# Where the weights of each TensorE pass stand in SBUF, modulo 256 bytes

## The chip, the cores and the metric

The kernel runs on one core of a Trainium2 chip. The metric is the device time of one execution in microseconds; before the change the median of three runs is 2378.27 us (2377.22 to 2378.45).

## The reference

Two layers of an encoder over 512 tokens of width 1024, all in float32. Each layer is a half-step SwiGLU, a mixer with three branches (chunked attention, pooling, forgetting attention), and a second SwiGLU; shift, scale and gate of each come from a vector `c`.

```python
for l in range(DEPTH):
    mod = (c_act @ w_ada[l] + b_ada[l]).reshape(B, N_MOD, D_MODEL)
    h = modulate(rms_norm(x, norm_gain[l, 0]), mod[:, 0], mod[:, 1])
    x = x + 0.5 * mod[:, 2][:, None, :] * swiglu(h, ffn_w_gate[l, 0], ffn_w_up[l, 0], ffn_w_down[l, 0])
    h = modulate(rms_norm(x, norm_gain[l, 1]), mod[:, 3], mod[:, 4])
    x = x + mod[:, 5][:, None, :] * hybrid_mixer(h, w_in[l], qk_gain[l], rel_bias[l], forget_bias[l], ...)
    h = modulate(rms_norm(x, norm_gain[l, 2]), mod[:, 6], mod[:, 7])
    x = x + 0.5 * mod[:, 8][:, None, :] * swiglu(h, ffn_w_gate[l, 1], ffn_w_up[l, 1], ffn_w_down[l, 1])
```

`swiglu(h, g, u, d)` is `(silu(h @ g) * (h @ u)) @ d` with an inner width of 2816.

## The kernel before

**Numbers in two halves.** Every float32 operand of a large product is split into a high half `hi` (a cast to the format that TensorE multiplies) and a low half `lo` (what the cast left over). A product is then three passes into the same accumulator: weights' hi by moving hi, weights' hi by moving lo, weights' lo by moving hi (L119 to L121 in `triple`, L128 to L130 in `add_product`). A pass is one load of 128 columns of weights and one matmul, with 512 moving columns ("wide") or 256 ("narrow").

**Weight chunks.** `wchunk` loads 512 KB of weights into a `raw` buffer (SP's queue), ACT casts them into `hi` (L291), and DVE subtracts to get `lo` (L293; at the very start POOL does). `hi` and `lo` come from two tags, `whi` and `wlo`, three buffers each, used in turn. At the boundary between two phases some chunks are fetched early into `ptb` or `b` buffers instead.

**Feed-forward.** Part of each gate and up product is formed wide, directly from chunks (`unit`). The rest is done two blocks at a time by `seven`, a scheme that needs seven products of quarter blocks in place of eight, all narrow: each has 12 passes. The blocks A11, A12 and A22 are split into `whi`/`wlo` buffers, and the sums and differences S1 to S4 into `ptb` buffers. In order the products are A11, A12, S2, S1, S3, S4, A22, so that over successive `seven` calls 36 passes with weights in `whi`/`wlo` alternate with 48 with weights in `ptb`. There are 70 calls. The down product runs through `k_outer` in wide passes, except for the last half of each phase, which runs in narrow ones, one half of the tokens after the other, so that the next norm can begin; the mixer's output product does the same.

**Mixer.** Query, key and value projections have the activations `hhi`/`hlo` as weights and the weight chunk as the moving operand, wide. In the attention, `weigh` (L1023, L1024) has the values (`xv`, `v2`) as weights and the transposed probabilities (`pta`, `ptb`) moving, narrow for the most part. `merge_units` and `pool_in` run wide from chunks.

**Order of the work.** PE's order is that in which the code emits its passes. Norm pieces, scheduled block sums and attention steps are put among them by `later` and `poll`, at counts of passes. On the other engines a scheduler orders the instructions within what their dependencies allow, and tags with a fixed number of buffers decide when a load or a cast may begin.

**Places in SBUF.** The table gives where the tiles of each tag begin in a partition, modulo 256 bytes, in the built program. A slice of 128 or 256 float32 columns steps by 512 or 1024 bytes, so all weights and moving slices of a tile share its value.

| Tag | before | after |
|---|---|---|
| `hhi`, `hlo`, `b`, `xv`, `v2` | 0 | 0 |
| `whi`, `wlo` (before), `w` (after) | 0 | 0, or 224 for slices taken with `NARROW` |
| `ptb` | 32 | 224 |
| `pta` | 96 | 32 |

The "distance" of a pass is the address of its weights minus that of its moving operand, modulo 256.

Of the kernel before, what the change touches and what calls it, by code (L numbers as in the profile page):

```python
# [15 lines left out]
F32 = mybir.dt.float32  # L16
F32R = mybir.dt.float32r
# [23 lines left out]
def encoder_kernel(tc, xT, c, w_ada, b_ada, gains, w_gate, w_up, w_down, w_qkv, w_f, w_ubg,  # L41
# [21 lines left out]

    def st(shape, dt, tag, bufs):
        return sb.tile(shape, dt, tag=tag, bufs=bufs, name=nm(tag))

    def acc(shape=(P, T)):
        return ps.tile(list(shape), F32, tag="acc", bufs=4, name=nm("acc"))
# [72 lines left out]
    nc.scalar.dma_start(crow, c)  # L141
    nc.scalar.activation(crow, crow, AF.Silu)
    x_blocks, squares, crows = [], [], []
    for b in range(4):
        xb = blk("xv", F32)
        nc.sync.dma_start(xb, xT[:, 2 * b:2 * b + 2, :])
        x_blocks.append(xb)
        sq = st([P, 2, T], F32, "wlo" if b else "whi", 3)
        for a in range(2):
            nc.scalar.activation(sq[:, a, :], xb[:, a, :], AF.Square)  # L150
        squares.append(sq)
        if b < 2:
            pc = mmt()
            mm(pc, ones[0:1, :], crow[:, b * T:(b + 1) * T], start=True, stop=True)
            crows.append(pc)
# [34 lines left out]
            yield  # L190


    modc = cp.tile([P, L, 9, KD], F32, name="modc")
    apre = cp.tile([P, L, 3, KD], F32, name="apre")

    def mod_step(l, j, d, tag="raw"):
        raw = st([P, D], F32, tag, {"v2": 4, "raw": NRAW, "b": NB}[tag])
# [75 lines left out]
                mod_credit[0] -= 1.0  # L273
                mod_pop()

    def wchunk(src, shape, side=True, spare=None, lo_eng=None):
        lo_eng = lo_eng or nc.vector
        side_work(side)
        raw = st([P] + list(shape), F32, *(("b", NB) if spare else ("raw", NRAW)))
        last["dma"] = nc.sync.dma_start(raw, src).ins  # L280
        if spare == "ptb":
            both = st([P, 2] + list(shape), F32R, "ptb", 2)
            hi, lo = both[:, 0], both[:, 1]
        elif spare == "b":
            hi = st([P] + list(shape), F32R, "b", NB)
            lo = st([P] + list(shape), F32R, "b", NB)
        else:
            hi = st([P] + list(shape), F32R, "whi", 3)
            lo = st([P] + list(shape), F32R, "wlo", 3)
        with behind("scalar"):  # L290
            nc.scalar.copy(hi, raw)  # L291
        with behind("vector"):
            lo_eng.tensor_tensor(lo, raw, hi.bitcast(F32), op=ALU.subtract)  # L293
        return hi, lo
# [107 lines left out]
    def k_outer(chunk_src, nch, lhs_rhs, before_last=None):  # L402

        if before_last is None:
            parts, nheld = [(None, slice(0, T), [acc() for _ in range(4)])], 2
        else:
            parts = [(hs, slice(hs * HALF, (hs + 1) * HALF), [b((P, HALF)) for _ in range(4)])
                     for hs, b in enumerate((mmt, acc))]  # L410
            nheld = 3

        def go(part, j, chunks):
            _, cols, accs = part
            for c, hi, lo in chunks:
                for kk in range(2):
                    a, b, x, y = lhs_rhs(hi[:, kk, :], lo[:, kk, :], 2 * c + kk, j)
                    triple(accs[j], a, b, x[:, cols], y[:, cols], start=(c == 0 and kk == 0),
                           stop=(c == nch - 1 and kk == 1))

        held = []
        for c in range(nch):
            if before_last is not None:
                if c == nch - 2:
                    quiet[0] = 8
                    before_last()
                quiet[0] = 8
            hi, lo = wchunk(chunk_src(c), (2, T))
            if c < nch - nheld:
                for part in parts:  # L430
                    for j in range(4):
                        go(part, j, [(c, hi, lo)])
            else:
                held.append((c, hi, lo))
        if before_last is not None:
            quiet[0] = 5
        for part in parts:
            for j in range(4):
                go(part, j, held[:-2])
            for j in range(4):  # L440
                go(part, j, held[-2:])
                yield j, part[0], part[2][j]
# [79 lines left out]
    def seven(srcs, blocks, bank):  # L522

        raws = []
        for src in srcs:
            side_work()
            raw = st([P, KD, P], F32, "raw", NRAW)
            last["dma"] = nc.sync.dma_start(raw, src).ins
            raws.append(raw)
        tens = lambda o, a, b, op: nc.vector.tensor_tensor(o, a, b, op=op)  # L530
        a11, a12, a21, a22 = raws[0][:, :4], raws[0][:, 4:], raws[1][:, :4], raws[1][:, 4:]
        ah, al = st([P, KD, P], F32R, "whi", 3), st([P, KD, P], F32R, "wlo", 3)
        split_to(ah, al, raws[0])
        bh, bl = st([P, 4, P], F32R, "whi", 3), st([P, 4, P], F32R, "wlo", 3)
        split_to(bh, bl, a22)
        s12, s34 = st([P, 2, 4, P], F32, "v2", 4), st([P, 2, 4, P], F32, "v2", 4)
        tens(s12[:, 0], a21, a22, ALU.add)
        minus(s34[:, 0], a11, a21)
        minus(s12[:, 1], s12[:, 0], a11)
        minus(s34[:, 1], a12, s12[:, 1])  # L540
        pair12, pair34 = st([P, 2, 2, 4, P], F32R, "ptb", 2), st([P, 2, 2, 4, P], F32R, "ptb", 2)
        split_to(pair12[:, 0], pair12[:, 1], s12)
        split_to(pair34[:, 0], pair34[:, 1], s34)
        lefts = {"A11": [(ah[:, k], al[:, k]) for k in range(4)],
                 "A12": [(ah[:, 4 + k], al[:, 4 + k]) for k in range(4)],
                 "A22": [(bh[:, k], bl[:, k]) for k in range(4)]}
        for name, pair, i in (("S1", pair12, 0), ("S2", pair12, 1), ("S3", pair34, 0), ("S4", pair34, 1)):
            lefts[name] = [(pair[:, 0, i, k], pair[:, 1, i, k]) for k in range(4)]
        x, y, w = bank((P, HALF)), bank((P, HALF)), bank((P, HALF))
        c = st([P, 4, HALF], F32, "v2", 4)  # L550
        go = lambda o, left, right, start: add_product(o, lefts[left], blocks.operand(right), start)
        go(x, "A11", "B11", True)
        nc.scalar.copy(c[:, 0], x)
        go(y, "A12", "B21", True)
        tens(c[:, 0], y, c[:, 0], ALU.add)
        go(x, "S2", "T2", False)
        nc.scalar.copy(c[:, 1], x)
        go(w, "S1", "T1", True)
        nc.scalar.copy(c[:, 2], w)
        go(x, "S3", "T3", False)  # L560
        nc.scalar.copy(c[:, 3], x)
        go(w, "S4", "B22", False)
        tens(c[:, 1], w, c[:, 1], ALU.add)
        tens(c[:, 3], c[:, 2], c[:, 3], ALU.add)
        go(x, "A22", "T4", False)
        return [[c[:, 0:2].rearrange("p a t -> p (a t)")], [x, c[:, 3]]]
# [334 lines left out]


    def forget(l):
        raw = st([P, KD, H], F32, "wf", 1)
        nc.sync.dma_start(raw, w_f[l])
        f2 = st([P, KD, 40], F32R, "ssum", 1)
        nc.gpsimd.memset(f2.bitcast(F32), 0.0)
        split_to(f2[:, :, :H], f2[:, :, 32:32 + H], raw)
        pf = mmt()
        for k in range(KD):  # L910
            poll()
            mm(pf[:40, :], f2[:, k, :], hhi[:, k, :], start=(k == 0), stop=False)
            mm(pf[:40, :], f2[:, k, :], hlo[:, k, :], start=False, stop=(k == KD - 1))
            pe[0] += 2.0
        z = t1(T)[:H, :]
        nc.scalar.copy(z, pf[32:32 + H, :])
        nc.vector.scalar_tensor_tensor(z, pf[:H, :], fbc[:, l:l + 1], z, op0=ALU.add, op1=ALU.add)
        a = t2(T)[:H, :]
        nc.vector.scalar_tensor_tensor(a, z, -1.0, z, op0=ALU.mult, op1=ALU.min)
        nc.scalar.activation(a, a, AF.Exp)  # L920
        nc.vector.tensor_scalar(a, a, 1.0, None, op0=ALU.add)
        nc.scalar.activation(a, a, AF.Ln)
        nc.vector.scalar_tensor_tensor(z, z, 0.0, a, op0=ALU.min, op1=ALU.subtract)
        cum = t2(T)[:H, :]
# [387 lines left out]
```

## Time and profile before

| | |
|---|---|
| median of three runs | 2378.27 us (2377.22 to 2378.45) |
| the profiled execution, its own time | 2379.88 us |
| its span, first to last instruction | 2378.1 us |
| granted TensorE clock, mean | 1.000 |
| PE busy | 2349.1 us, 99% |
| DVE busy | 1768.0 us, 74% |
| ACT busy | 1200.3 us, 50% |
| POOL busy | 333.9 us, 14% |
| HBM traffic | 134 GB/s over the span |

PE is TensorE's matmuls, PEld its weight loads, which overlap them; DVE is VectorE, ACT is ScalarE, POOL is GpSimd, SP the engine that issues most loads. Matmuls are pipelined: the duration of one in the profile is longer than the time until the next begins. A line number is one of the kernel before.

### The profile page before, as it was taken

What the parts mean: (1) busy time and instruction counts of PE and PEld (TensorE: products, weight loads), DVE (VectorE), ACT (ScalarE), POOL (GpSimd) and SP (SyncE); (2) the same over time, 40 slices, a digit from 0 to 9 for tenths busy, and PEclk for the clock granted to TensorE, in tenths of its full rate; (3) what the DMA queues carried; (4) which work ended last, traced back from release to release, by engine and by line L of the source; (5) the groups of instructions that cost most, each with busy time, mean ns of one, the idle gap of its engine ahead of it and who ended that gap; (6) DMA issues with size and microseconds to landing.
All of it is one profiled execution on the core that took longest, in us unless ns stands there. A gap on an engine that the chain in (4) does not pass through costs nothing.

```text
span 2378.1 us, 37464 instructions
## 1 busy us (share of the span) xinstructions
PE 2349.1 (99%) x14322; PEld 2092.7 (88%) x14322; DVE 1768.0 (74%) x3147; ACT 1200.3 (50%) x2097; POOL 333.9 (14%) x433
## 2 busy tenths in 40 slices
PE   7999999999999999999999999999999999999999
PEld 5899998878888898989999989988888888999898
DVE  8887876787685577878677878677866855878583
ACT  5353554676632363535553636456765324636262
POOL 3000011244412210000000000122543222000000
PEclk9999999999999999999999999999999999999999
DMA  7535343333355524353415353533343654243333
GB/s 279 193 107 186 94 164 95 107 98 109 116 194 211 186 72 160 110 183 107 151 63 171 101 190 107 186 107 99 95 124 106 223 202 159 68 136 107 99 103 100
DMA packets 117975, 325.16 MB, mean 137 GB/s; under 512 B 11650, under 2 KB 13826, under 8 KB 117796
## 3 DMA queue, kind: packets, MB, share of 16 engines
q1 hardware_dynamic: 115106, 314.38, 40.0%
q0 software_dynamic: 2688, 8.39, 1.2%
q8 instruction: 112, 1.84, 0.3%
q14 instruction: 67, 0.55, 0.1%
q10 hardware_dynamic: 2, 0.00, 0.0%
HBM read 312.16 MB, written 6.38 MB: 134 GB/s over the span
## 4 chain that ended last, share of the span: by engine, by line
PE 89%; DVE 6%; ACT 2%; issue 1%; DMA 1%; POOL 0%; DVEq 0%; ACTq 0%; POOLq 0%
PE acc L119 16%; PE acc L121 16%; PE acc L120 16%; PE mm L128 5%; PE mm L129 5%; PE mm L130 5%; PE acc L128 5%; PE acc L129 5%; PE acc L130 5%; PE mm L119 3%; PE mm L121 3%; PE mm L120 3%; PE mm L1001 1%; DVE v L206 1%; PE mm L1024 1%
## 5 line engine op out<-in xcount | busy, mean ns | idle before, releaser
L291 ACT CAST whi<-raw 128x1024 fp32r<-128x1024 f32 (+1 forms) x255 | 264.8, 1042 | 385.6 <-PE acc L120 255.3
L293 DVE TENSOR_TENSOR wlo<-raw,whi 128x1024 fp32r<-128x1024 f32 x247 | 303.8, 1233 | 155.6 <-ACT whi L291 142.8
L119 PE MATMUL acc<-b,whi 128*128 128x512 f32 (+1 forms) x960 | 360.7, 376 | 0.0
L120 PE MATMUL acc<-b,whi 128*128 128x512 f32 (+1 forms) x960 | 357.4, 372 | 0.0
L121 PE MATMUL acc<-b,wlo 128*128 128x512 f32 (+1 forms) x960 | 357.0, 372 | 0.0
L121 PEld LDWEIGHTS acc<-b,wlo 128*128 128x128 f32 x960 | 181.0, 189 | 31.5
L119 PEld LDWEIGHTS acc<-b,whi 128*128 128x128 f32 x960 | 181.0, 189 | 30.1
L120 PEld LDWEIGHTS acc<-b,whi 128*128 128x128 f32 x960 | 181.1, 189 | 29.6
L399 DVE TENSOR_TENSOR ptb<-v,ptb 128x1024 fp32r<-128x1024 f32 x140 | 171.2, 1224 | 37.6 <-ACT ptb L398 35.7
L398 ACT CAST ptb<-v 128x1024 fp32r<-128x1024 f32 x140 | 146.6, 1050 | 100.0 <-DVE v L467 52.2
L119 PE MATMUL acc<-hhi,whi 128*128 128x512 f32 x480 | 192.0, 401 | 2.5 <-ACT hhi L728 1.7
L120 PE MATMUL acc<-hlo,whi 128*128 128x512 f32 x480 | 188.5, 393 | 2.4 <-DVE hlo L731 2.4
L121 PE MATMUL acc<-hhi,wlo 128*128 128x512 f32 x480 | 188.4, 393 | 1.3 <-DVE wlo L293 1.3
L398 ACT CAST whi<-raw 128x1024 fp32r<-128x1024 f32 (+1 forms) x140 | 116.7, 834 | 118.7 <-PE acc L120 54.0
L119 PE MATMUL acc<-whi,hhi 128*128 128x512 f32 x336 | 138.8, 414 | 1.0 <-ACT t L830 0.9
L399 DVE TENSOR_TENSOR wlo<-raw,whi 128x1024 fp32r<-128x1024 f32 (+1 forms) x140 | 133.2, 951 | 8.8 <-ACT whi L398 7.4
L121 PE MATMUL acc<-whi,hlo 128*128 128x512 f32 x336 | 132.0, 393 | 0.0
L120 PE MATMUL acc<-wlo,hhi 128*128 128x512 f32 x336 | 131.7, 392 | 0.0
L206 DVE CUSTOM_DVE_ANT_0 v<-v,b,badac 128x1024 f32<-128x1024 f32 x87 | 116.3, 1344 | 14.7 <-DMA v<-in_w_ada_dram 14.6
L448 DVE SCALAR_TENSOR_TENSOR xv<-acc,modc,xv 128x512 f32<-128x512 f32 (+1 forms) x112 | 77.0, 690 | 56.2 <-PE acc L121 56.0
L129 PE MATMUL mm<-b,ptb 128*128 128x256 f32 x420 | 118.3, 282 | 0.0
L129 PE MATMUL acc<-b,ptb 128*128 128x256 f32 x420 | 118.3, 282 | 0.0
(313 smaller groups left out, 6660.3 us busy)
## 6 DMA issues: line engine op xcount, KB each, us to landing
raw<-in_w_down_dram SPq DMA_DIRECT2D x88, 512.0 KB, 4.1
v<-in_w_ada_dram SPq DMA_DIRECT2D x87, 512.0 KB, 5.3
raw<-in_w_up_dram SPq DMA_DIRECT2D x82, 512.0 KB, 3.6
raw<-in_w_gate_dram SPq DMA_DIRECT2D x79, 512.0 KB, 3.6
b<-in_w_ada_dram SPq DMA_DIRECT2D x57, 512.0 KB, 5.1
raw<-in_w_ubg_dram SPq DMA_DIRECT2D x56, 512.0 KB, 3.7
raw<-in_w_qkv_dram SPq DMA_DIRECT2D x42, 512.0 KB, 3.7
raw<-in_w_branch_dram SPq DMA_DIRECT2D x24, 512.0 KB, 3.6
```

What stands on the lines that cost most here:

```text
L119: mm(o, lh, rh, start=start, stop=False)
L120: mm(o, lh, rl, start=False, stop=False)
L121: mm(o, ll, rh, start=False, stop=stop)
L128: mm(o, lh, rh, start=start and k == 0, stop=False, skip_group_check=True)
L129: mm(o, lh, rl, start=False, stop=False, skip_group_check=True)
L130: mm(o, ll, rh, start=False, stop=k == 3, skip_group_check=True)
L206: dot = nc.vector.tensor_tensor_reduce(out=raw, in0=raw, in1=silc[0], scale=1.0, scalar=badac[:, l, j, d:d + 1], op0=ALU.mult, op1=ALU.add ...
L291: nc.scalar.copy(hi, raw)
L293: lo_eng.tensor_tensor(lo, raw, hi.bitcast(F32), op=ALU.subtract)
L398: nc.scalar.copy(hi, src)
L399: nc.vector.tensor_tensor(lo, src, hi.bitcast(F32), op=ALU.subtract)
L448: nc.vector.scalar_tensor_tensor(x, acc_j, gate, x, op0=ALU.mult, op1=ALU.add)
```

## The change

A helper `duo` gives both halves of a chunk from one buffer. The tag `w` (three buffers of 8448 bytes a partition) takes the place of `whi` and `wlo` (three of 4096 each); the halves begin at 0 and 4096 bytes, or 224 bytes (56 float32) further with `place=NARROW`. `seven` takes its A11, A12 and A22 with `NARROW`, `wchunk` does in the narrow half of `k_outer`. A tile `pad` of 192 bytes is put ahead of `ptb`, which moves from 32 to 224. So narrow passes with weights in `w` or `ptb` go to distance 224; the attention's passes that have `ptb` as the moving operand go from 224 to 32.

Room is made by writing the adaLN results `modc` and `apre` over the tables `badac` and `gainc` that they are made from, by giving the load of `w_f` the `yl` buffer of the attention in place of its own `wf`, and by putting the four squares of the start into two `w` buffers.

```diff
+    WIDE, NARROW = 0, 56
+
+    def duo(shape, tag="w", place=WIDE):
+
+        if tag == "ptb":
+            st([P, 48], F32, "pad", 1)
+            t, place = st([P, 4 * T], F32R, tag, 2), 0
+        else:
+            t = st([P, 4 * T + 64], F32R, tag, 3)
+        n = int(np.prod(shape))
+        parts = []
+        for base in (0, 2 * T):
+            v = t[:, base + place:base + place + n]
...
+            parts.append(v)
+        return parts
...
+    sq_parts = duo((2, T)) + duo((2, T))
...
-        sq = st([P, 2, T], F32, "wlo" if b else "whi", 3)
+        sq = sq_parts[b].bitcast(F32)
...
-    modc = cp.tile([P, L, 9, KD], F32, name="modc")
-    apre = cp.tile([P, L, 3, KD], F32, name="apre")
+    modc, apre = badac, gainc
...
-    def wchunk(src, shape, side=True, spare=None, lo_eng=None):
+    def wchunk(src, shape, side=True, spare=None, lo_eng=None, place=WIDE):
...
         if spare == "ptb":
-            both = st([P, 2] + list(shape), F32R, "ptb", 2)
-            hi, lo = both[:, 0], both[:, 1]
+            hi, lo = duo(shape, "ptb")
...
         else:
-            hi = st([P] + list(shape), F32R, "whi", 3)
-            lo = st([P] + list(shape), F32R, "wlo", 3)
+            hi, lo = duo(shape, "w", place)
...
-            hi, lo = wchunk(chunk_src(c), (2, T))
+            hi, lo = wchunk(chunk_src(c), (2, T), place=WIDE if before_last is None else NARROW)
...
-        ah, al = st([P, KD, P], F32R, "whi", 3), st([P, KD, P], F32R, "wlo", 3)
+        ah, al = duo((KD, P), "w", NARROW)
...
-        bh, bl = st([P, 4, P], F32R, "whi", 3), st([P, 4, P], F32R, "wlo", 3)
+        bh, bl = duo((4, P), "w", NARROW)
...
-        pair12, pair34 = st([P, 2, 2, 4, P], F32R, "ptb", 2), st([P, 2, 2, 4, P], F32R, "ptb", 2)
+        pair12, pair34 = duo((2, 4, P), "ptb"), duo((2, 4, P), "ptb")
...
-        raw = st([P, KD, H], F32, "wf", 1)
+        raw = st([P, KD, H], F32, "yl", 1)
```

The order of PE's passes stays as it was but for one place per layer in the attention, where a few neighbours trade places. Two places on other engines move. On SP before, the load of layer 1's `w_f` (`wf`) stands among the query, key and value weights of layer 0's mixer:

```order
L280 DMA raw_3531<-in_w_down_dram 128x2x512
L280 DMA raw_3537<-in_w_down_dram 128x2x512
L280 DMA raw_3879<-in_w_qkv_dram 128x2x512
L280 DMA raw_3967<-in_w_qkv_dram 128x2x512
L905 DMA wf_16639<-in_w_f_dram 128x64
L280 DMA raw_4020<-in_w_qkv_dram 128x2x512
L280 DMA raw_4053<-in_w_qkv_dram 128x2x512
```

Now it stands at the start of the merge of layer 0, as `yl`, between a branch weight and a gate weight (`in_w_ubg_dram`):

```order
L1225 DMA b_7052<-sil_dram 128x1024
L300 DMA raw_7169<-in_w_ubg_dram 128x1024
L1119 DMA t_1366_7054<-in_w_pool_dram 128x4x128
L300 DMA raw_7225<-in_w_branch_dram 128x2x512
L923 DMA yl_16479<-in_w_f_dram 128x64
L300 DMA raw_7236<-in_w_ubg_dram 128x1024
L300 DMA raw_7341<-in_w_ubg_dram 128x1024
```

It has moved past all the loads of layer 0's attention, and the gate weights of the merge are now behind it in SP's queue.

On DVE, in the first feed-forward, there is a weight's low half (`wlo`, line L293), with two adaLN dots (L206) behind it, before:

```order
L467 TENSOR_TENSOR v_123_599<-v_123_599 128x2x256
L293 TENSOR_TENSOR wlo_670<-raw_667,whi_669 128x1024
L206 ISA v_133_665,modc<-v_133_665,b_73,badac 128x1024
L206 ISA modc 128x1
L206 ISA v_149_744,modc<-v_149_744,b_73,badac 128x1024
L206 ISA modc 128x1
L217 TENSOR_SCALAR modc<-modc 128x1
L492 TENSOR_TENSOR v_153_761<-hhi,hlo 128x1024
```

After the change the low half (`w`, L311 there) has one of the two dots (L226) ahead of it:

```order
L485 TENSOR_TENSOR v_109_583<-v_109_583 128x2x256
L226 ISA v_118_648,badac<-v_118_648,b_73,badac 128x1024
L226 ISA badac 128x1
L311 TENSOR_TENSOR w_652<-raw_650,w_652 128x1024
L237 TENSOR_SCALAR badac<-badac 128x1
L510 TENSOR_TENSOR v_136_742<-hhi,hlo 128x1024
L226 ISA v_133_726,badac<-v_133_726,b_73,badac 128x1024
L226 ISA badac 128x1
```

The second dot has moved behind the next block sum (`hhi`, `hlo`). Such swaps of neighbours are found in many places on DVE, ACT and SP.

More of the change, by code (lines that the diff above doesn't have):

```diff
@@ L65, in st @@
         return sb.tile(shape, dt, tag=tag, bufs=bufs, name=nm(tag))
+    WIDE, NARROW = 0, 56
[9 more added lines that the diff above has]
+            v = t[:, base + place:base + place + n]
+            if len(shape) == 2:
+                v = v.rearrange("p (a b) -> p a b", a=shape[0])
+            elif len(shape) == 3:
+                v = v.rearrange("p (a b c) -> p a b c", a=shape[0], b=shape[1])
+            parts.append(v)
+        return parts
     def acc(shape=(P, T)):
@@ L540, in seven @@
         minus(s34[:, 1], a12, s12[:, 1])
-        pair12, pair34 = st([P, 2, 2, 4, P], F32R, "ptb", 2), st([P, 2, 2, 4, P], F32R, "ptb", 2)
-        split_to(pair12[:, 0], pair12[:, 1], s12)
-        split_to(pair34[:, 0], pair34[:, 1], s34)
+        pair12, pair34 = duo((2, 4, P), "ptb"), duo((2, 4, P), "ptb")
+        split_to(*pair12, s12)
+        split_to(*pair34, s34)
         lefts = {"A11": [(ah[:, k], al[:, k]) for k in range(4)],
@@ L547, in seven @@
         for name, pair, i in (("S1", pair12, 0), ("S2", pair12, 1), ("S3", pair34, 0), ("S4", pair34, 1)):
-            lefts[name] = [(pair[:, 0, i, k], pair[:, 1, i, k]) for k in range(4)]
+            lefts[name] = [(pair[0][:, i, k], pair[1][:, i, k]) for k in range(4)]
         x, y, w = bank((P, HALF)), bank((P, HALF)), bank((P, HALF))
```

## The prediction

> **What bounds the kernel now.** I read the page first, then the table of who waited for whom on PE, then the groups of instructions with their shapes kept apart, and last the busy times of hand-picked stretches, in which start-to-start times can be counted.
>
> ```profile
> span 2378.1 us, 37464 instructions
> PE 2349.1 (99%) x14322; PEld 2092.7 (88%) x14322; DVE 1768.0 (74%) x3147; ACT 1200.3 (50%) x2097; POOL 333.9 (14%) x433
> PE 89%; DVE 6%; ACT 2%; issue 1%; DMA 1%; POOL 0%; DVEq 0%; ACTq 0%; POOLq 0%
> ```
>
> PE is busy for 99% of the span and carries 89% of the chain that ended last. The table of waits on PE says how much it stood still:
>
> ```profile
> PE mm L717 <- ACT ssum L712: 4.7, 1, 4.7
> ...
> PE acc L120 <- DVE hlo L731: 2.4, 2, 1.4
> PE acc L119 <- ACT hhi L728: 1.7, 1, 1.7
> PE acc L121 <- DVE wlo L293: 1.3, 3, 0.5
> ```
>
> The table begins with the longest: 4.7 us, once, in the opening. Behind it PE hardly waits for anything, so a pass that is shorter by some nanoseconds is a shorter kernel, as long as the other engines keep up. The price of a pass is not the mean in the groups (a 256-column matmul shows about 282 ns, but the next one starts long before that). It is the time from one start to the next, which I get from stretches that begin at the first pass of a run and end at the start of the pass behind it.
>
> Which passes change place? The groups, with shapes kept apart (a row for each of the two accumulator pools and each of the three passes of a product; I show one of each kind):
>
> ```profile
> L128 PE MATMUL mm<-b,ptb 128*128 128x256 f32 x420 | 118.1, 281 | 0.1
> ...
> L128 PE MATMUL mm<-hhi,whi 128*128 128x256 f32 x280 | 79.4, 283 | 0.0
> ...
> L119 PE MATMUL mm<-b,whi 128*128 128x256 f32 x160 | 45.4, 284 | 0.2 <-ACT whi L291 0.2
> ...
> L128 PE MATMUL mm<-b,whi 128*128 128x256 f32 x140 | 39.6, 283 | 0.4 <-ACT v L561 0.4
> L128 PE MATMUL mm<-hhi,ptb 128*128 128x256 f32 x140 | 39.6, 283 | 0.0
> ...
> L119 PE MATMUL mm<-hhi,ptb 128*128 128x256 f32 x96 | 24.6, 282 | 0.0
> ...
> L119 PE MATMUL acc<-ptb,hhi 128*128 128x512 f32 x32 | 13.0, 407 | 0.0
> ...
> L1023 PE MATMUL mm<-ptb,v 128*128 128x256 f32 x48 | 12.3, 286 | 0.0
> ...
> L119 PE MATMUL mm<-v,whi 128*128 128x256 f32 x32 | 9.1, 283 | 0.0
> ```
>
> In a row the moving tile stands ahead of the weights. By the addresses of the built program all moving tiles of these rows but `ptb` begin at 0 modulo 256, `whi` and `wlo` too, and `ptb` at 32. So weights in `whi`/`wlo` stand at distance 0: three lines times two pools times (280 + 140 + 160 + 32) = 3672 passes. Weights in `ptb` stand at distance 32: three lines times (two pools times (420 + 140), and 96) = 3648 passes. All 7320 go to 224. The attention's 192 passes of L1023 and L1024 with `ptb` moving under `v` or `xv` go the other way, from 224 to 32, and 96 wide passes of L119 to L121 (`ptb` moving under `hhi` or `hlo`) too. The other wide passes, 5612 at distance 0, stay.
>
> **The change part by part.** First the price at distance 0 and at 32. Both lie side by side in one stage of the seven-product scheme: runs of 36 passes with weights in `whi`/`wlo`, and between them runs of 48 with weights in `ptb`. Seven runs of the first kind, then eight of the second (first columns: stretch, its length, PE busy):
>
> ```profile
> core 0: us, PE busy (x), PEclk, DMA share, GB/s
> 1083.61:1087.91 4.30, 4.30 (x38) 1.00 0.37 142
> ...
> sum 30.15, PE 30.15; mean PE 4.31
> ```
>
> ```profile
> 1077.93:1083.61 5.68, 5.68 (x51) 5.68 (x50) 4.80 (x7) 2.71 (x5) 0.00 (x0) 1.00 0.24 84
> ...
> sum 45.39, PE 45.39 PEld 45.39 DVE 40.25 ACT 21.38 POOL 0.00; mean PE 5.67 PEld 5.67 DVE 5.03 ACT 2.67 POOL 0.00
> ```
>
> The count in brackets takes in the neighbours that reach into the stretch; the passes that start in it are 36 and 48. So 30.15 us / 252 = 119.6 ns at distance 0, and 45.39 us / 384 = 118.2 ns at 32, at a granted clock of 1.00 in both. Lengths of a first run (4.30 and 5.68) and means (4.31 and 5.67) differ by 0.01 us, so each kind repeats itself closely.
>
> The price at 224 in long runs is not in this trace. The nearest rows are the attention's weighted sums, six passes in a row with `v` or `xv` as weights over `ptb`; here six such groups:
>
> ```profile
> 596.37:597.07 0.70, 0.70 (x7) 1.00 0.69 281
> ...
> sum 4.20, PE 4.20; mean PE 0.70
> ```
>
> 4.20 us / 36 = 116.7 ns. The other row at 224 is of wide passes. Here 96 of them at distance 0 stand ahead of a stretch of 12 at 224:
>
> ```profile
> 1154.90:1176.68 21.78, 21.78 (x98) 18.04 (x97) 11.42 (x13) 11.43 (x15) 2.24 (x2) 1.00 0.39 132
> 374.76:377.56 2.80, 2.80 (x14) 2.26 (x13) 2.80 (x9) 2.29 (x6) 1.70 (x4) 1.00 0.06 22
> ```
>
> 226.9 ns at 0 against 233.3 ns at 224: a wide pass loses 6.4 ns there. The bounds for a narrow pass at 224 are therefore 119.6 + 6.4 / 2 = 122.8 ns above, and half a wide pass at its best, 113.4 ns, below. I take 116.7, since that row has the same width and the same distance.
>
> The terms, with minus for a gain. Passes from 0: 3672 x (119.6 - 116.7) = -10.7 us (ends -22.8 and +11.8). Passes from 32: 3648 x (118.2 - 116.7) = -5.5 us (ends -17.5 and +16.8). The attention's 192: +0.3 us, with the same price difference. The 96 wide ones: no long row at 32, so between their price at 0 (-0.6) and no gain; I take -0.3.
>
> A rule of the skill speaks against the whole term. The Trainium skill, "TensorE: Matmul & The Clock Gate", section "Step-by-step: what each phase is for", has two independent read ports for PE, one for the moving operand and one for the weights, and says that loading the next weights takes no read bandwidth from the running matmul. By that rule the distance would be worth nothing, and the sum would be 0 instead of -16. The 119.6 against 118.2 ns above, same shape, stage and clock, don't agree with it, though other things than the address differ between `whi` and `ptb`.
>
> Does another engine become late? In a whole stage of 672 such passes DVE has the most to do (columns: PE, PEld, DVE, ACT, POOL):
>
> ```profile
> 1075.06:1154.90 79.84, 79.84 (x674) 79.83 (x673) 69.69 (x107) 46.84 (x81) 0.00 (x0) 1.00 0.41 130
> ```
>
> The stage would shrink by 288 x 2.9 + 384 x 1.5 ns = 1.4 us, to 78.4; DVE needs 69.7. It stays ahead. At the five boundaries between phases, narrow passes cover the next norm's chain on ACT and DVE, and PE waits there at some already (the rows of L120 and L119 above). If none of the saved time of 96 passes (0.3 us) counted at any of the five, 1.4 us would be lost; I take +0.5.
>
> The halves of a weight chunk now share one buffer, so ACT's cast may begin only after the last pass of the old chunk, L121 or L130, instead of L120 or L129: one pass later.
>
> ```profile
> L291 ACT CAST whi<-raw 128x1024 fp32r<-128x1024 f32 (+1 forms) x255 | 264.8, 1042 | 385.6 <-PE acc L120 255.3
> ```
>
> ACT stands at this wait for 255 us already and PE lost 1.3 us to `wlo` in the row above: three buffers in turn put a chunk ready long before its use. One pass, 0.12 to 0.23 us, costs nothing under that cover; if the cover were gone, 255 casts at 0.2 us would cost 50 us. What is queued behind the cast on ACT are evacuations, which PE waits for only through an accumulator.
>
> The load of `w_f` for layer 1 leaves its own buffer for that of `yl`, so SP's queue waits at it until the attention's last read of `yl` on POOL, with the weight loads of the merge queued behind:
>
> ```profile
> 655.75 0.74 POOL L1030 TENSOR_TENSOR b<-yl,b 64x256 fp32r<-64x256 f32 x1 [1.37 <-ACT b L1029]
> ```
>
> ```profile
> 659.70 0.34 SPq L280 DMA_DIRECT2D raw<-in_w_ubg_dram  x1
> ```
>
> POOL's read ends at 656.5 and the next load behind it left at 659.7: 3.2 us of cover, so 0. The swaps of neighbours on DVE (an adaLN dot ahead of a weight's low half) shift that half by one dot; the three buffers cover that too. Table aliases (`modc` into `badac`, `apre` into `gainc`) and the squares' new place change no instruction: 0. For all the moved issues together I keep 0, with +3 as an end, about what PE lost to weights and norms so far.
>
> Sum: -10.7 - 5.5 + 0.3 - 0.3 + 0.5 = -15.7 us. The profiled execution took 2379.88 us; it becomes 2364.2. It stands 1.6 above the median of the three runs (2378.27), so the forecast for the median is 2362.6 us.
>
> **The rivals.** *The distance is not the cause.* The 1.4 ns between `whi` and `ptb` rows, and the 116.7 of the attention, come from something else, such as the short run or the same weights loaded twice over. For it: the groups at 224 are only six long and begin behind other work. Against it: eight runs of 48 and seven of 36, all alike. The time would be 2378.3 us. This is also the case in which the rule of two ports holds.
>
> *Slower: 224 hurts narrow passes in long runs as it hurts wide ones.* A narrow pass pays half of the wide one's 6.4 ns on top of 119.6. Then 3672 x 3.2 + 3648 x 4.6 = +28.5 us, 2407 us. It decides for slower once a long run at 224 costs more than (119.6 + 118.2) / 2 = 118.9 ns. For it: the wide rows. Against it: those 12 passes have other weights (`hhi`) and DVE busy throughout, and the attention's 36 narrow passes at the very distance are faster than both.
>
> *Faster still: 224 takes all of the extra away*, and a narrow pass costs half a wide one at its best, 113.4 ns: -40 us, 2338 us. Against it: the attention's rows would have shown it.
>
> **How the numbers follow.** Forecast 0.76, no cause 0.09, slower 0.08, faster still 0.07. The prediction is the likeliest, 2362.6 us; its own range is 2355 to 2370 (117.7 to 115.7 ns for a narrow pass). From 2350 to 2378.3 the range takes in one half of the case of no cause and leaves out the slower one and most of the fastest, some 0.2 together. A difference below 0.2% (4.8 us) is about what a measurement of this kernel can't tell from none. Faster: 0.76 + 0.07 = 0.83; within: 0.09; slower: 0.08.
>
> **What would show it.** Runs of the seven-product scheme should lose their two prices: 48 passes in 5.60 us instead of 5.67, 36 in 4.20 instead of 4.31, the stage of 672 in 78.4 instead of 79.84. Wide runs should stay at 226.9 ns, PE's waits in sum as they are. The forecast is wrong if the stage takes over 79.6 us, or if it shrinks while waits on `w` or a raw load turn up on PE.

## The result and the profile after

The changed kernel takes 2369.19 us, the median of six runs (2367.45 to 2370.37). The kernel before, beside it, takes 2378.36 us (six runs, 2377.22 to 2380.35). The ratio is 0.996, with a 95% interval from 0.9947 to 0.9973: 9.2 us faster. The forecast of 2362.6 us had the direction right, the range held the time, near its upper end of 2370, and the gain was 6.6 us smaller than forecast.

The page of the kernel after: span, engines, and the chain that ended last.

```profile
span 2365.7 us, 37435 instructions
PE 2336.6 (99%) x14322; PEld 2077.1 (88%) x14322; DVE 1771.6 (75%) x3147; ACT 1198.3 (51%) x2097; POOL 325.8 (14%) x433
PE 89%; DVE 6%; ACT 2%; DMA 1%; issue 1%; POOL 0%; SPq 0%; ACTq 0%; DVEq 0%; POOLq 0%
```

The span fell by 12.4 us and PE's busy time by 12.5. The number of passes and the other engines' work are as before. PE still carries the chain.

Now the stage from which the forecast took its prices, in the kernel after. Columns: stretch, its length, PE busy, clock, DMA share, GB/s. First two runs of 36 passes with weights in `w`, then two of 48 with weights in `ptb`:

```profile
1077.07:1081.27 4.20, 4.20 (x38) 1.00 0.46 143
1086.87:1091.07 4.20, 4.20 (x38) 1.00 0.36 129
```

```profile
1081.27:1086.87 5.60, 5.60 (x50) 1.00 0.30 94
1091.07:1096.67 5.60, 5.60 (x51) 1.00 0.15 30
```

36 passes in 4.20 us and 48 in 5.60 are 116.7 ns each: what the prediction named, to the last digit. The stage as a whole, one run of 48 in it, and the 96 wide passes behind it (columns after the length: PE, PEld, DVE, ACT, POOL busy):

```profile
1068.67:1147.43 78.76, 78.74 (x673) 78.54 (x672) 69.38 (x107) 46.69 (x81) 0.00 (x0) 1.00 0.40 130
1110.71:1116.49 5.78, 5.76 (x51) 5.56 (x49) 5.30 (x9) 3.09 (x6) 0.00 (x0) 1.00 0.13 29
1147.43:1169.21 21.78, 21.78 (x99) 18.02 (x97) 11.53 (x13) 11.58 (x15) 2.25 (x2) 1.00 0.37 137
```

The wide passes did not move: 21.78 us, as before. But the stage of 672 took 78.76 us where 78.4 was forecast, and the run of 48 passes in the middle row took 5.78 us instead of 5.60. The missing part of the gain begins here. The waits on PE of the kernel after (us in total, times, longest):

```profile
PE mm L735 <- ACT ssum L730: 4.5, 1, 4.5
...
PE acc L141 <- DVE w L311: 1.8, 3, 0.7
PE acc L139 <- ACT hhi L746: 1.7, 1, 1.7
PE acc L148 <- ACT v L579: 1.5, 5, 0.5
PE acc L140 <- DVE hlo L749: 1.1, 1, 1.1
```

Of the norm's waits, ACT's stayed at 1.7 us and DVE's fell from 2.4 to 1.1; the wait for DVE's half of the weights grew a little (1.8 us against 1.3). One row grew more. Before it was

```profile
PE acc L128 <- ACT v L561: 0.4, 1, 0.4
```

and now it has 1.5 us, five times: PE waits for ACT's copy of an accumulator (L579, the same copy as L561 before).

The table names only part of the waits, so I also counted all gaps between the starts of PE's passes, over the whole trace. No single row shows these sums. I call what a narrow gap of over 135 ns has above 118 ns a stall, and the rest clean.

| us over the whole kernel | before | after |
|---|---|---|
| narrow passes, clean | 925.4 | 910.2 |
| narrow passes, stalls | 10.2 | 12.9 |
| of these, in the seven-product stages | 3.0 | 6.5 |
| wide passes, clean | 1313.0 | 1313.8 |
| wide passes, stalls | 30.9 | 30.4 |

In the seven-product stages 14 stalls (4.4 us) of the kernel after lie where A22 begins behind S4. Before there were 4 there (1.6 us). The table of waits names only a part of these. Here is one stall of the kernel after, with PE first, then ACT, DVE, and the queue of SP that issues the raw loads (start, duration, engine, line, out<-in, idle time before and who ended it):

```profile
1347.83 0.28 PE L150 MATMUL mm<-hhi,ptb 128*128 128x256 f32 x1
1348.37 0.39 PE L148 MATMUL mm<-b,w 128*128 128x256 f32 x1 [0.26 <-ACT v L579]
```

```profile
1346.99 1.05 ACT L416 CAST ptb<-v 128x1024 fp32r<-128x1024 f32 x1 [1.27 <-DVE v L485]
1347.94 0.37 ACT L579 COPY v<-mm 128x256 f32<-128x256 f32 x1
```

```profile
1342.93 0.69 DVE L548 TENSOR_TENSOR v<-raw 128x512 f32<-128x512 f32 x1 [2.16 <-DMA raw<-in_w_gate_dram]
...
1346.94 0.69 DVE L485 TENSOR_TENSOR v<-raw,v 128x512 f32<-128x512 f32 x1
```

```profile
1325.35 1.62 SPq L546 DMA_DIRECT2D raw<-in_w_up_dram  x2
1336.03 1.62 SPq L546 DMA_DIRECT2D raw<-in_w_gate_dram  x2
```

Read from the end: the A22 product adds into an accumulator that ACT must copy out first (an evacuation, L579). The copy stands in ACT's queue behind the cast of the next call's S1 and S2 (L416), whose DVE sums came late. All 14 stalls have this form: right ahead of the copy is that cast, and the cast had waited 0.9 to 1.6 us for DVE's sum (L485).

In the stall shown DVE had waited 2.16 us for a raw load. It is the only one of the 14 of that kind. In the other 13 DVE had worked for 9.6 us without a pause when the sum was due. DVE's work is not even: every second call also carries products of the SwiGLU (L623) and the splitting of their result. Here are a lighter call and the heavier one behind it, from last sum to last sum; the stall at the end of the middle row above (1110.71 to 1116.49) follows them (columns: stretch, length, DVE busy):

```profile
1095.17:1104.38 9.21, 7.69 (x12) 1.00 0.35 116
1104.38:1115.06 10.68, 10.16 (x17) 1.00 0.29 99
```

One call is 84 passes, 9.8 us of PE's time at 116.7 ns, and was 10.0 us at the old prices. DVE's 10.2 us of work in the heavier call fit into neither, and in the lighter one DVE waited 1.0 us for a raw load, so it could not get ahead. Such a load leaves only when DVE has done with the buffer: SP waited 99 times, 411 us in all, for L485 ahead of these loads, and the two shown left 10.7 us apart. The pair of calls took DVE 19.9 us, where two calls of PE take 19.6 now and took 20.0 before. That fits the stalls, but no run varied DVE's work alone.

In the kernel before, at the same call as the stall shown, ACT waited a quarter as long:

```profile
1355.03 1.05 ACT L398 CAST ptb<-v 128x1024 fp32r<-128x1024 f32 x1 [0.36 <-DVE v L467]
1355.99 0.36 ACT L561 COPY v<-mm 128x256 f32<-128x256 f32 x1
```

So the theory after the result is: the price of a pass depends on the distance as forecast, and the rest of the gain was lost to a chain from DVE's sums, late by their own load of work or by a late raw load, over ACT's cast to an evacuation queued behind it. The rivals are that the moved buffers and loads cost it, or that the price of long runs isn't set by the distance.

### The profile page after: what moved, and what is told of

Same layout as the page of the kernel before. It is cut to its first block, busy times and chain, and to the rows that moved or that the text cites. A ratio compares the mean times of both kernels' runs of the same rounds, so it can differ in the third digit from the quotient of the medians.

```text
span 2365.7 us, 37435 instructions
## 1 busy us (share of the span) xinstructions
PE 2336.6 (99%) x14322; PEld 2077.1 (88%) x14322; DVE 1771.6 (75%) x3147; ACT 1198.3 (51%) x2097; POOL 325.8 (14%) x433
## 4 chain that ended last, share of the span: by engine, by line
PE 89%; DVE 6%; ACT 2%; DMA 1%; issue 1%; POOL 0%; SPq 0%; ACTq 0%; DVEq 0%; POOLq 0%
PE acc L139 16%; PE acc L141 16%; PE acc L140 16%; PE acc L148 5%; PE mm L149 5%; PE mm L150 5%; PE mm L148 5%; PE acc L149 5%; PE acc L150 5%; PE mm L141 3%; PE mm L139 3%; PE mm L140 3%; PE mm L1019 1%; DVE v L226 1%; DVE w L311 1%
## 5 line engine op out<-in xcount | busy, mean ns | idle before, releaser
L311 DVE TENSOR_TENSOR w<-raw,w 128x1024 fp32r<-128x1024 f32 x247 | 313.0, 1271 | 163.8 <-ACT w L309 163.6
L309 ACT CAST w<-raw 128x1024 fp32r<-128x1024 f32 (+1 forms) x255 | 264.4, 1041 | 275.5 <-PE acc L141 191.4
L139 PE MATMUL acc<-b,w 128*128 128x512 f32 (+1 forms) x960 | 359.8, 375 | 0.0
L141 PE MATMUL acc<-b,w 128*128 128x512 f32 (+1 forms) x960 | 356.3, 371 | 0.0
L140 PE MATMUL acc<-b,w 128*128 128x512 f32 (+1 forms) x960 | 356.3, 371 | 0.0
L141 PEld LDWEIGHTS acc<-b,w 128*128 128x128 f32 x960 | 180.3, 188 | 31.8
L139 PEld LDWEIGHTS acc<-b,w 128*128 128x128 f32 x960 | 180.3, 188 | 30.1
L140 PEld LDWEIGHTS acc<-b,w 128*128 128x128 f32 x960 | 180.4, 188 | 29.8
L416 ACT CAST ptb<-v 128x1024 fp32r<-128x1024 f32 x140 | 147.0, 1053 | 97.1 <-DVE v L485 58.2
L139 PE MATMUL acc<-hhi,w 128*128 128x512 f32 x480 | 191.8, 401 | 2.6 <-ACT hhi L746 1.7
L141 PE MATMUL acc<-hhi,w 128*128 128x512 f32 x480 | 188.4, 393 | 1.8 <-DVE w L311 1.8
L140 PE MATMUL acc<-hlo,w 128*128 128x512 f32 x480 | 188.2, 392 | 1.1 <-DVE hlo L749 1.1
L416 ACT CAST w<-raw 128x1024 fp32r<-128x1024 f32 (+1 forms) x140 | 116.5, 832 | 120.7 <-PE acc L141 56.0
L417 DVE TENSOR_TENSOR w<-raw,w 128x1024 fp32r<-128x1024 f32 (+1 forms) x140 | 133.4, 953 | 13.2 <-ACT w L416 13.2
L139 PE MATMUL acc<-w,hhi 128*128 128x512 f32 x336 | 138.8, 414 | 0.8 <-ACT t L848 0.8
L140 PE MATMUL acc<-w,hhi 128*128 128x512 f32 x336 | 131.7, 392 | 0.0
L141 PE MATMUL acc<-w,hlo 128*128 128x512 f32 x336 | 131.7, 392 | 0.0
L226 DVE CUSTOM_DVE_ANT_0 v<-v,b,badac 128x1024 f32<-128x1024 f32 x87 | 116.7, 1351 | 11.6 <-DMA v<-in_w_ada_dram 11.3
L466 DVE SCALAR_TENSOR_TENSOR xv<-acc,badac,xv 128x512 f32<-128x512 f32 (+1 forms) x112 | 77.4, 691 | 54.8 <-PE acc L141 54.7
```

The lines of the kernel that those rows point to most:

```text
L139: mm(o, lh, rh, start=start, stop=False)
L140: mm(o, lh, rl, start=False, stop=False)
L141: mm(o, ll, rh, start=False, stop=stop)
L226: dot = nc.vector.tensor_tensor_reduce(out=raw, in0=raw, in1=silc[0], scale=1.0, scalar=badac[:, l, j, d:d + 1], op0=ALU.mult, op1=ALU.add ...
L416: nc.scalar.copy(hi, src)
L417: nc.vector.tensor_tensor(lo, src, hi.bitcast(F32), op=ALU.subtract)
```

## The experiments

Times are medians; each ratio is to the kernel before, run on the same chip, with its 95% interval. Edits are those to the kernel after unless said otherwise.

### Both distances back, all else as changed

```diff
-    WIDE, NARROW = 0, 56
+    WIDE, NARROW = 0, 0
...
-            st([P, 48], F32, "pad", 1)
```

> Both go back, w to 0 and ptb to 32; the shared buffers, the aliased tables and the place of w_f stay as changed. Theory: all narrow prices as before the change and the rest neutral, 2377 to 2380, same as before. Rival (shared buffers and moved issues gain by themselves): 2370. Second rival (they cost, and ate part of the gain): 2381 to 2384.

2377.18 us, ratio 0.999 (0.9981 to 0.9999). Runs of 36 with weights in `w`, then of 48 with weights in `ptb`:

```profile
1081.82:1086.13 4.31, 4.31 (x39) 1.00 0.41 138
1076.15:1081.82 5.67, 5.67 (x51) 1.00 0.36 105
```

Both old prices are back (119.7 and 118.1 ns). Shared buffers, aliased tables and the moved load cost nothing; they may even gain a little, as the interval lies just below 1. This kernel differs from the kernel after in the two distances alone, and the two intervals (0.9981 to 0.9999, 0.9947 to 0.9973) don't meet: 0.3%, some 7 us of the 9.2, is what the distances gave. The stalls in the seven-product stages fell from 3.0 to 2.1 us. With the distances the same kernel has 6.5 us of stalls there, so it is the shorter passes that bring them.

### One distance at a time

Weights in `w` at 0, only `ptb` moved:

```diff
-    WIDE, NARROW = 0, 56
+    WIDE, NARROW = 0, 0
```

> Only the narrow weights in w go back from 224 to 0; ptb stays at 224. Theory (each narrow pass is priced by its distance, 119.6 ns at 0, 118.2 at 32, 116.85 at 224): 3672 passes pay 2.8 ns more, some of it returned by smaller stalls, so 8 to 10 us over the changed kernel's 2369, 2377 to 2379; a run of 36 passes takes 4.31 us again, one of 48 stays at 5.61. Rival (the gain comes from the shared buffers and the moved issues, not the distance): stays at 2369, a run of 36 at 4.21.

Weights in `ptb` at 32, only `w` moved:

```diff
-            st([P, 48], F32, "pad", 1)
```

> Only ptb goes back from 224 to 32; narrow weights in w stay at 224. Theory: 3648 passes pay 1.35 ns more, 3 to 5 us over the changed kernel's 2369, 2372 to 2374; a run of 48 takes 5.67 us again, one of 36 stays at 4.21. Rival (not the distance): 2369, a run of 48 at 5.61.

The first took 2376.07 us, ratio 0.9984 (0.9975 to 0.9993), the second 2371.25 us, ratio 0.9965 (0.9953 to 0.9978). Runs of 36 and 48 in the first kernel, then in the second:

```profile
1081.30:1085.61 4.31, 4.31 (x38) 1.00 0.43 137
1075.69:1081.30 5.61, 5.61 (x50) 1.00 0.34 105
```

```profile
1078.89:1083.09 4.20, 4.20 (x39) 1.00 0.43 141
1073.21:1078.89 5.68, 5.68 (x50) 1.00 0.34 105
```

Each price moves with its own address and not with the other's. The two times lie 0.9 and 0.8 us below the ranges that were expected. By time alone the first kernel can't be told from the one with both back, since their intervals overlap; the share of `ptb` is read from the passes. Against the kernel with both back, clean narrow time falls by 4.6 us with `ptb` alone, by 10.1 with `w` alone, by 15.2 with both; the terms forecast were 5.5 and 10.7. The stalls rise each time (7.3 us with both back; 9.3, 10.7, 12.9).

### Eight distances for the narrow weights in `w`

```diff
+        calls[0] += 1
+        place = 8 * (calls[0] % 8)
-        ah, al = duo((KD, P), "w", NARROW)
+        ah, al = duo((KD, P), "w", place)
-        bh, bl = duo((4, P), "w", NARROW)
+        bh, bl = duo((4, P), "w", place)
```

> The weights of A11, A12 and A22 in the seven-product scheme take the eight distances 0, 32, ... 224 in turn, a call each; ptb stays at 224. Theory: start-to-start time follows the distance alone, 119.6 ns at 0, 118.2 at 32, 116.85 at 224, and what lies between is open; 224 need not be the best. Rival (only the tag of the weights counts): all eight alike.

One run, 2372.09 us. Means of all clean narrow passes of the kernel, by their distance:

| distance | 0 | 32 | 64 | 96 | 128 | 160 | 192 | 224 |
|---|---|---|---|---|---|---|---|---|
| ns | 119.2 | 118.3 | 115.5 | 118.8 | 119.1 | 119.7 | 117.8 | 117.0 |

At 0, 32 and 224 passes that don't take turns are in the mean too; those that do cost 119.6, 118.2 and 117.5 ns there. Runs of 24 passes (A11 and A12) at 0, 32 and 64, and 12 at 64 (A22):

```profile
1120.36:1123.22 2.86, 2.86 (x26) 1.00 0.42 152
1130.26:1133.10 2.84, 2.84 (x27) 1.00 0.16 63
1140.38:1143.21 2.83, 2.83 (x27) 1.00 0.94 324
1148.82:1150.19 1.37, 1.37 (x14) 1.00 0.93 348
```

The lowest are 64 and, by some way behind it, 224 and 192. But 64 doesn't have one price: in the same call 24 passes cost some 118 ns each and the 12 of A22 some 114. That led to the runs at 64 below.

### The moving operand moved instead

`hhi` and `hlo` begin at 32, narrow weights in `w` at 0, `ptb` at 32. So weights in `w` over `hhi` stand at 224, without their own address having changed, and the wide passes over `hhi` too.

```diff
+    cp.tile([P, 8], F32, name="shift")
...
+    cp.tile([P, 56], F32, name="restore")
-    WIDE, NARROW = 0, 56
+    WIDE, NARROW = 0, 0
-            st([P, 48], F32, "pad", 1)
```

> Weights in w at 0 and ptb at 32 as before the change, but hhi and hlo, the moving operand, stand at 32 instead of 0. So narrow passes of w over hhi or hlo are at 224 without the weights having moved, narrow passes of ptb over hhi or hlo are at 0, and those over b keep 0 and 32. Theory (the difference of the two addresses counts): 116.8 ns for w over hhi, 119.7 for ptb over hhi, 119.7 for w over b, 118.2 for ptb over b; wide passes of w over hhi slow down from 227 to 233 ns, so the kernel takes some 10 us more. Rival (the address of the weights itself counts): 119.7 for all with w, 118.2 for all with ptb, wide ones unchanged.

One run, 2388.04 us. Weights in `w` over `hhi` and `hlo` at 224 (24 passes), weights in `ptb` over `hhi` at 0 (12):

```profile
1078.85:1081.65 2.80, 2.80 (x26) 1.00 0.50 139
1088.75:1091.58 2.83, 2.83 (x26) 1.00 0.26 104
1095.84:1097.27 1.43, 1.43 (x14) 1.00 1.04 338
```

116.7 and 117.9 ns at 224, 119.2 at 0: it is the difference of the two addresses that counts, since the same `w` at 0 costs less once the moving operand stands at 32, and the same `ptb` at 32 more. Between two runs at 224 lies 1.2 ns, so it is not the difference alone. Wide passes over `hhi` cost 233 ns here, which is what makes the kernel slower than before.

That 256 bytes is the period can be read from the kernel after. Its three `w` buffers lie 8448 bytes apart, so of the clean narrow passes at 224, by the addresses of the built program, 6086 stand at 224 modulo 512 and 1209 at 480: 116.86 and 116.81 ns.

### Eight distances for the wide weights

```diff
+            if place == WIDE:
+                calls[0] += 1
+                place = 8 * (calls[0] % 8)
             hi, lo = duo(shape, "w", place)
```

> The changed kernel, with the chunks that serve wide passes at the eight places 0, 32, ... 224 in turn, a chunk each; narrow weights stay at 224. Theory (a wide pass is at its best at distance 0, 227 ns, and costs 5 to 7 ns more elsewhere, as the 96 passes at 224 and at 32 did): 7 of 8 of some 4500 passes pay 5 to 7 ns, 20 to 28 us over the changed kernel. Rival (those 96 passes were slow for what surrounds them): all eight near 227 ns, time as the changed kernel.

One run, 2390.36 us, 21 us above the kernel after. 24 wide passes at 64:

```profile
1229.81:1235.41 5.60, 5.60 (x26) 1.00 0.52 178
```

That is 233.3 ns; the clean means over the kernel are 229.8 at 0 (in the long runs at 0 alone it was 226.9), 230.1 at 192, and 232.7 to 233.6 at the six others. Leaving the wide ones at 0 was right, and a distance that suits the narrow ones does not suit the wide.

### The copy of the accumulator ahead of the cast

The cast of the next call's S1 and S2 is told to issue behind this call's copy `c[:, 3]`. Nothing else is changed.

```diff
+        with tc.issue_after(copied[0]) if copied else contextlib.nullcontext():
+            nc.scalar.copy(pair12[0], s12)
+        minus(pair12[1], s12, pair12[0].bitcast(F32))
-        split_to(*pair12, s12)
...
-        nc.scalar.copy(c[:, 3], x)
+        copied[:] = [nc.scalar.copy(c[:, 3], x).ins]
```

> The changed kernel, with one order on ACT: the cast of the next call's S1 and S2 into ptb is issued behind the copy of the S3 accumulator instead of ahead of it. Theory (the stalls ahead of A22 come from that copy, which stands in ACT's queue behind a cast that waits for DVE): the 14 stalls between S4 and A22, 4.4 us, vanish nearly all, and the kernel takes 3 to 5 us less than the changed one, 0.9945 to 0.995 of the kernel before. Rival (the load and block-sum loop is slower than PE in these stages, so the stall only moves to another product): the same sum of stalls, ahead of S2 or A11, and no gain.

2363.86 us, ratio 0.9935 (0.9922 to 0.9949). No kernel of the study is faster, and the gain over the kernel after, 5.3 us between the medians, is a little above the 3 to 5 that were expected. Its interval just touches that of the kernel after (0.9947 to 0.9973); its five runs (2362.36 to 2366.12 us) all lie below the six of that kernel. No stall is left where A22 begins; 2.6 us in four stalls now lie where S2 begins. In all the stages have 3.5 us of stalls instead of 6.5, and all narrow passes 9.2 instead of 12.9. The engines on its page, from its waits the one that is left at S2 (L575 is the copy of A11's product, `c[:, 0]`), and ACT at the longest of them:

```profile
PE 2332.6 (99%) x14322; PEld 2075.9 (88%) x14322; DVE 1766.9 (75%) x3147; ACT 1200.1 (51%) x2097; POOL 327.3 (14%) x433
```

```profile
PE mm L148 <- ACT v L575: 2.0, 2, 1.7
```

```profile
1483.26 1.04 ACT L309 CAST w<-raw 128x1024 fp32r<-128x1024 f32 x1 [2.04 <-DMA raw<-in_w_down_dram]
1484.21 0.36 ACT L575 COPY v<-mm 128x256 f32<-128x256 f32 x1
```

So it is the same pattern with another copy and another cast: S2 adds into the accumulator that L575 must copy, and in all four stalls that copy stands behind the cast of a weight chunk that had waited for its raw load. PE's busy time is 4.0 us below that of the kernel after, with as many instructions on every engine and nearly the same work (DVE 1766.9 us against 1771.6, ACT 1200.1 against 1198.3).

The same edit in the kernel before, to see whether it was worth this much all along:

> The kernel before the change, with the copy ahead of the cast and nothing else. Theory (the copy's place is a stall of its own, which the shorter passes make larger): its four stalls ahead of A22 go, 1.6 us, 0.999 of the kernel before, much less than the 5 us that the same order gives the changed kernel. Rival (the order is worth 5 us with any distance): 0.998 or below.

2378.37 us, ratio 0.9993 (0.9984 to 1.0002): not told from nothing. The four stalls ahead of A22 are gone here too, and the seven-product stages have 1.3 us of stalls instead of 3.0, but narrow stalls elsewhere grew, and in all there are 10.8 us instead of 10.2. By the medians the queue order cost about 1 us while passes were longer, and some 5 us once they were shorter. The two gains (0.07% and 0.25%) have intervals that overlap, so that the order costs more with shorter passes rests on the traces: 1.7 us fewer stalls in these stages there, 3.0 here.

### Narrow weights at 64

```diff
-    WIDE, NARROW = 0, 56
+    WIDE, NARROW = 0, 16
...
-            st([P, 48], F32, "pad", 1)
+            st([P, 8], F32, "pad", 1)
```

> The changed kernel with all the narrow weights at distance 64 in place of 224. Theory (price by distance; 115.5 ns at 64 in the run with eight distances, 116.85 at 224): 7320 passes save 1.4 ns, 10 us, of which stalls in the seven-product stages take back 3 to 5: 5 to 7 us under the changed kernel, 0.993 to 0.994 of the kernel before. Rival (64 was good only among other distances): 116.9 ns or more, no gain over the changed kernel.

With the copy ahead of the cast as well:

> Distance 64 and the copy ahead of the cast together. Theory: the full 10 us of the shorter passes and 4 us or more of the stalls, 0.990 to 0.992 of the kernel before. Rival (load loop is the bound): as with 64 alone.

The first took 2368.95 us, ratio 0.9955 (0.9943 to 0.9968), the second 2364.01 us, ratio 0.9937 (0.9924 to 0.9949): no better than 224 in either form, and short of the 0.993 to 0.994 and 0.990 to 0.992 that were expected. The reason is in three runs of 36 passes, all with weights in `w` at 64, of the second kernel:

```profile
1077.41:1081.65 4.24, 4.24 (x38) 1.00 0.40 135
1087.11:1091.19 4.08, 4.08 (x39) 1.00 0.27 104
1106.37:1110.45 4.08, 4.08 (x38) 1.00 0.50 184
```

One distance has two steady prices, 117.8 and 113.3 ns, and keeps the one or the other for several runs. Of 129 unbroken runs of 36 or 48 passes 29 were at the low one in the first kernel, and 55 in the second. What the shorter passes save comes back as stalls: against the kernel with the copy first at 224, the second kernel has 3.4 us less of clean narrow time, and 14.9 us of narrow stalls instead of 9.2, 4.5 of them where S2 begins, behind the copy L575.

### Taking work off DVE

If DVE's sums are late, POOL, which is idle in the stage shown above, could form one of the four. This is the kernel with the copy first, and

```diff
-        minus(s34[:, 0], a11, a21)
+        nc.gpsimd.tensor_tensor(s34[:, 0], a11, a21, op=ALU.subtract)
```

> The copy ahead of the cast as before, and one of the four block sums of each seven-product call (A11 - A21) on POOL instead of DVE. Theory (what stalls are left come from DVE's chain behind the load): 0.6 us less for DVE in each of 70 calls, the stalls in the seven-product stages sink below 2 us, 2 us or so under the kernel with the copy ahead alone. Rival (POOL and DVE get in each other's way, and POOL takes over 2 us for what took DVE 0.7): no gain or slower by a few us.

2402.38 us, ratio 1.0096 (1.0083 to 1.011). The groups of POOL's sum, of DVE's three that are left, the first of these in the kernel with the copy first and nothing on POOL, and the wait on PE with POOL's sum:

```profile
L558 POOL TENSOR_TENSOR v<-raw,raw 128x512 f32<-128x512 f32 x70 | 116.9, 1670 | 1012.4 <-DMA raw<-in_w_gate_dram 680.2 <-DMA raw<-in_w_up_dram 156.8 <-DVE ptb L417 133.1
L550 DVE TENSOR_TENSOR v<-raw 128x512 f32<-128x512 f32 x70 | 62.1, 888 | 39.4 <-DMA raw<-in_w_gate_dram 36.1 <-DMA raw<-in_w_up_dram 3.2
L485 DVE TENSOR_TENSOR v<-v,raw 128x512 f32<-128x512 f32 x70 | 60.2, 860 | 1.0
L485 DVE TENSOR_TENSOR v<-raw,v 128x512 f32<-128x512 f32 x70 | 48.0, 685 | 1.3
```

```profile
L550 DVE TENSOR_TENSOR v<-raw 128x512 f32<-128x512 f32 x70 | 48.3, 690 | 40.5 <-DMA raw<-in_w_gate_dram 37.2 <-DMA raw<-in_w_up_dram 3.1
```

```profile
PE mm L148 <- ACT v L575: 26.8, 26, 2.4
```

Here POOL needs 1670 ns for what DVE does in 690, and two of DVE's own sums take 860 and 888; its last one stays at 685. PE loses 33 us in 30 stalls where S2 begins. In 27 of them the copy L575 stands behind the cast of a weight chunk that had waited for its raw load, as above. That the raw buffers are held longer is the likely link, but it isn't shown. The Trainium skill, "SBUF — State Buffer", section "Who interferes with whom", has a DVE instruction with two SBUF inputs contend with one of GpSimd that reads SBUF. The trace agrees for DVE (690 to 860 and 888 ns); what POOL would take alone no run shows. So the rival was right that work moved off DVE gains nothing, though not in size: it expected a few us, and the kernel is some 38 us slower than with the copy alone. A third raw buffer would be another way to loosen the chain. It wasn't tried: the tiles of this kernel leave no room for its 4096 bytes a partition.

## Why the prediction was right, and where it was not

**Prices at 0 and 32.** Right. The kernel with both distances back has them to 0.1 ns.

**Price at 224.** Right in kind and nearly in size: 116.7 ns in the undisturbed runs, 116.85 over the kernel. The 0.15 ns cost 1.1 us (7320 passes). Nearly all of it (1008 passes x 1.1 ns = 1.1 us) comes from 24 of the 129 unbroken runs of 36 or 48 passes, which cost 117.8 ns a pass, such as this one of 48 in the kernel after:

```profile
1363.38:1369.04 5.66, 5.66 (x51) 1.00 0.93 315
```

That six short groups of the attention gave the price of long runs to the digit was in part luck: the mean of all the attention's clean passes at 224 was 117.2 ns in the kernel before.

**Distance as the cause.** Right. The rival that something else makes the 1.4 ns falls with the kernels that move one address and nothing else. With it the rule of two ports that the prediction cites (the Trainium skill, "TensorE: Matmul & The Clock Gate", section "Step-by-step: what each phase is for") falls as a reason to expect no gain: with the same work and clock, 36 passes take 4.31 or 4.20 us by where the weights stand.

**224 hurts narrow passes as it hurts wide ones.** Wrong for the narrow ones, and the wide ones do lose 6 ns at 224, as the runs with eight distances and with the moving operand moved show. *Faster still*, 113.4 ns, did not come at 224. That price exists, at 64, in a part of the runs.

**Shared buffers, `w_f`, aliases, moved issues.** Right at 0: ratio 0.999 with both distances back.

**The wide 96 and the attention.** The 96 at 32 cost 232.8 ns, where 233.4 stood before: the -0.3 us was nothing. The attention's 192 rose from 117.2 to 118.3 ns, 0.2 us for the forecast's 0.3. All wide passes together came out 0.3 us longer.

**The step that failed** is the one on DVE: "The stage would shrink to 78.4; DVE needs 69.7. It stays ahead." A busy sum over a stage says whether an engine has time for its work in the mean, not whether a result is there when it is due. In every second call DVE has 10.2 us to do where PE now takes 9.8, and in 13 of the 14 stalls it had worked for 9.6 us without a pause. Then everything behind it on ACT, in order, was late too. The prediction had looked at that queue: "What is queued behind the cast on ACT are evacuations, which PE waits for only through an accumulator." It put this at nothing, and the accumulator is where PE waited. Its sign of being wrong, waits on `w` or a raw load on PE, was near but named another path. The kernel with the copy first shows the path: with as many instructions on DVE and ACT, the order alone gives back some 5 us (0.25% between the ratios, 4.6 us between all starts of PE's passes). The price of the step is the rise of narrow stalls, 2.7 us in the kernel after against the 0.5 us that the prediction held for the norms. Measured from the kernel with both distances back, where the stalls were 7.3 us, it is 5.6 us; the new structure had saved 2.9 first, which wasn't forecast either.

**The sum.** The profiled execution was forecast at 2364.2 us and took 2367.45, 3.3 us more: 2.2 from stalls, 0.6 from wide passes, 0.7 from the clean narrow passes in sum (rounded). The other 3.3 us of the miss are no term at all. The forecast took 1.6 us off, since the profiled execution of before lay so far above its median; that of after lies 1.7 us below its own. Half of the miss is thus chance in which executions were profiled.

## What to carry to other kernels

Measure a pass from start to start in stretches of one kind, and place its weights for its own width: here 224 and 64 bytes were the best of eight distances for 256 columns, and both cost 512 columns more than 0 does (233 ns against 227 to 230). When the passes of a kernel get shorter, look at every in-order queue for an evacuation that PE needs soon and that stands behind an instruction waiting for a load or for a late engine, and put the evacuation first. Read slack call by call, from when a result is due, not from the busy share of a stage.

## What the runs showed that was not expected

A pass has not one price at a distance but, at 64 and at 224, two: 113.3 and 117.8 ns, and 116.7 and 117.8 ns. (In the kernel with eight distances the runs of 24 show two at 96 as well, 117.4 and 120.1, and at 128, 118.4 and 120.1.) In the kernel after, all ten changes from one to the other between neighbouring runs fall on a wait of PE (the longest gap in them is 198 to 816 ns); 16 other waits changed nothing, and in 92 neighbouring pairs without a wait the price never changed. In the kernel with the copy first, which has no wait at A22, the higher price doesn't occur in any run of 36 or 48, and clean narrow time is 1.2 us shorter. At 64, in the kernel with the copy first, five of eleven changes fell on gaps of only 123 or 124 ns. So a wait can cost more than its own length, through the price of what comes behind it. That PE can be kept at 113.3 ns, some 25 us over 7320 passes below 116.7, was not shown; what in a wait decides, and what in the memory or the engine lies behind the distance, stays open.
